# Attention's PSUM as four single banks and two pairs instead of two and three

## The chip, the cores and the metric

The kernel runs on one core of one Trainium2 chip. The metric is the device time of one execution in microseconds (us), as the median of three runs. An execution is 39,685 instructions on five engines that run side by side and wait for each other by semaphores: TensorE (PE in the profile), VectorE (DVE), ScalarE (ACT), GpSimd (POOL) and SyncE (SP, which here issues the transfers).

## The reference

Two layers of a network with four branches are computed for 512 latent and 128 context tokens of width 1024. Each layer is

```
h = modulate(rms_norm(x, g_attn), sh1, sc1)
cb, cc, cv, gq, gk, gv, nq, nk, nv, mq, mkv, mkr, gates = in_project(h, w_in)
y_conv = short_conv(cb, cc, cv)
y_gqa  = banded attention of 8 heads on 2 key heads, with a sink per head
y_na   = neighbourhood attention of 4 heads, with a bias table per head
y_mla  = attention of 4 heads on compressed keys and values
x = x + gt1 * (sum of gate_i * (y_i @ w_branch_i)) @ w_o
x = x + gt2 * relu(modulate(rms_norm(x, g_mlp), sh2, sc2) @ w_ff1)^2 @ w_ff2
```

The keys and values of every attention branch also take in 256 cached tokens. All of it is float32; the outputs are the two normed token sets and the new caches.

## The kernel before

Tokens lie on the free axis (640 of them, worked on in two halves of 320), features on the 128 partitions. Each weight slab of 128 columns is split into a high and a low part, so that a projection of one half is 8 steps of three matmuls (`steps`, L199 to L201: high by high, high by low, low by high), all added up in one PSUM tile of one bank.

PSUM has eight banks. `psum(n1, n2)` (L96) opens two pools for a phase: n1 single banks, from which `bank()` takes a tile named `pr`, and n2 pairs of neighbouring banks, from which `banks2()` takes a tile that the profile calls `S`. A tile that takes over a bank waits until the last instruction that reads the bank's tile before it has ended. All phases but one use eight single banks. The attention phase of each layer (`mixers`, L656) uses two singles and three pairs (L680).

What the attention phase does with them: `attend` (L610) goes through 80 blocks, each one head's 128 queries (16 heads of five blocks, the fifth the context's own). A block passes three places:

- `block_scores` takes a pair and writes the scores into it (L479, L480, or L482 to L484 for the MLA heads). VectorE writes the sink column (L508) and takes the row minimum together with the mask table (L515, or L518 without a table); ScalarE's exponential (L524) is the last to read the pair. GpSimd then divides by the sum (L529). Scores are three blocks ahead.
- `block_T` takes a pair and transposes the block's probabilities into it (L538). ScalarE copies their high part out (L542), VectorE subtracts it for the low part (L545), which is the last read of the pair.
- `pair_pv` takes a single bank for the product of two blocks with the values (L555), read out by ScalarE (L559) and VectorE (L578, L576 or L568). It is called from within a projection, after its third step (L202).

Between them `fill` runs pieces of the projections still to come: half of a block's share between the transposition and the next scores, half after them. Each half projection takes a single bank and is read out by ScalarE (L299, L300 and others) or VectorE. The MLA heads' preparation (L1351, L1362, L1383), the sums of squares (L1220) and their spreading (L1239) take single banks as well. `v_pair` takes a pair for three transpositions of values per layer (L414).

The order on TensorE is that of the program text. On VectorE, ScalarE and GpSimd it is chosen in the attention phase by a scheduler when the program is built, by when it reckons their inputs to be ready; within an engine the order is then fixed, and an instruction that waits holds up all that stand behind it. Which of the free banks a new tile gets is settled there too.

Of the kernel before, what the change touches and what calls it, by code (L numbers as in the profile page):

```python
# [36 lines left out]
# slabs of w_in, 128 columns each (MKR: 32), and of the MLA heads' second projections (HEAD + i);  # L37
# the order in which they are used after GK, GQ, GV
# [4 lines left out]
# gate, first row chunk and number of chunks of its branch's projection; first chunk of y  # L43
# [3 lines left out]
# TensorE time to fill per attention block (GQA, neighbourhood, MLA), and the MLA preparation's steps  # L47
RATE = (2000, 2200, 2000)
PREP = (820, 600, 1200)
# blocks scored ahead; share of a block's filling before the next scores; blocks by which the  # L50
# product with the values lags, and the step of a projection under which it runs
AHEAD, PART, LAG, FRESH = 3, 0.5, 1, 2
# blocks to wait for the inputs of the values' transposition, of the norms' sums, of their spreading
# [12 lines left out]
class Net:  # L66
# [28 lines left out]
    @contextmanager  # L95
    def psum(self, n1, n2=0):  # L96
        """PSUM for one phase: n1 single banks, n2 pairs of banks"""
        self.uid += 1
        with ExitStack() as s:
            pool = lambda name, n: s.enter_context(  # L100
                self.tc.tile_pool(name=f"{name}_{self.uid}", bufs=n, space=PSUM, reuse_waits="tile"))
            self.ps1 = pool("ps1", n1)
            self.ps2 = pool("ps2", n2) if n2 else None
            yield
# [35 lines left out]
    def raw(self):  # L140
        """start the load of the next slab"""
        src, kc, m, tag, eng = self.feed.popleft()
        r = self.wp.tile([P, kc, m], F32, name="raw" + tag, tag="raw" + tag, bufs=2 if tag == "w" else 1)
        self.nc.sync.dma_start(r, src.rearrange("p (k m) -> p k m", k=kc))
        self.raws.append((r, kc, m, tag, eng))

    def prefetch(self, dst=None):
        """split the next slab; start the load of the one after it"""
# [9 lines left out]
        if eng and kc == KC:  # L158
            # in halves, so that no engine is held for long
            for a, e in ((0, nc.gpsimd), (KC // 2, nc.vector)):  # L160
                c = slice(a, a + KC // 2)
                nc.scalar.copy(hi[:, c], raw[:, c])
                e.tensor_tensor(lo[:, c], raw[:, c], _r(hi[:, c]), ALU.subtract)
        else:
            nc.scalar.copy(hi, raw)  # L165
            nc.vector.tensor_tensor(lo, raw, _r(hi), ALU.subtract)  # L166
# [4 lines left out]
    def take(self, ahead=True, dst=None):  # L171
        """the next slab; by default the one after it is split meanwhile"""
        if not self.ready:
            self.prefetch()
        hi, lo, tag = self.ready.popleft()
        if ahead:
            self.look(tag)
        return hi, lo

    def look(self, last="w"):  # L180
        """split what comes next, up to a large slab; never two small ones, which share a buffer"""
# [10 lines left out]
    def steps(self, out, w, x, sl, ks=None):  # L192
        """out += sum_k w[k]^T x[k], both operands split; a step per k, yields its time on TensorE"""
# [32 lines left out]
    def silu(self, pool, a, n):  # L226
        """a <- silu(a), n columns"""
# [15 lines left out]
    def mod_chunk(self):  # L243
        """128 modulation columns of both vectors, on VectorE"""
# [11 lines left out]
    def mod_done(self, l, i0, i1):  # L256
        """add the bias to columns i0..i1; fold the norm's gain into 1 + scale"""
# [10 lines left out]
    def mod_first(self, pool, j, w):  # L268
        """layer 0's first shift and scale, chunk j, on TensorE: rows of both vectors, then columns"""
# [19 lines left out]
    def evac(self, ps, h, raw, rows, scale, perm, ctx0):  # L289
        """a PSUM half -> raw[rows, lat 512 | ... | ctx at ctx0]; perm: grid order (r, b, c) -> (b, r, c)"""  # L290
# [23 lines left out]
    def stage(self):  # L314
        """a staging tile; work put off that reads the tile it takes over runs first"""
# [12 lines left out]
    # work put off: small pieces run between the attention blocks, in order  # L328
# [3 lines left out]
    def drain(self, budget=None, tasks=None):  # L332
        """run work put off: all of it, or up to a budget, or all that these tasks have left"""
# [8 lines left out]
    # the same for work on TensorE: one piece per block, once its inputs have had time to arrive  # L342
# [26 lines left out]
    def q_pair(self, raw, rope):  # L369
        """two heads: per head the stack of q_hi (the head's own rows) and q_lo"""  # L370
# [16 lines left out]
    def k_pair(self, raw, rope):  # L387
        """two heads: per head k_hi and k_lo, each in both halves of the partitions"""
# [17 lines left out]
    def v_pair(self, raw):  # L406
        """two heads, token-major values [V_hi | V_lo]; chunks: lat 0-3, ctx 4, cache 5-6"""
# [18 lines left out]
    def wait(self, begun=0, ended=0):  # L426
        """hold a fill task until so many heads have begun and ended"""
# [3 lines left out]
    def q_prep(self, c, rope, perm, out):  # L431
        """fill task: a query chunk"""
# [40 lines left out]
    # A block is one head's 128 queries. Three parts, run for different blocks at a time:  # L473
    # scores and softmax; transposition of the probabilities; product with the values.
# [11 lines left out]
    def block_scores(self, B):  # L486
# [8 lines left out]
        # the sink is one more column of scores  # L495
# [51 lines left out]
    def pair_pv(self, R):  # L547
        """[V_hi P; V_lo P] of a pair of blocks"""
# [31 lines left out]
    def values_out(self):  # L580
        """the pending product with the values. It takes the bank of the last projection: best soon
        after the next one has begun, which leaves both time to be read out"""
# [5 lines left out]
    def blocks(self, H):  # L588
        """the blocks of a head: latent queries in two pairs, then the context's own"""
# [20 lines left out]
    def attend(self, blocks, fill, budget):  # L610
        """software pipeline over the blocks; projections fill TensorE in between"""
# [32 lines left out]
    def na_table(self, l, head, piece):  # L644
        """a piece of a neighbourhood head's table: BIG outside the column window, less the bias;
        zeros for the cached keys are there already"""
# [8 lines left out]
    def mixers(self, l, first):  # L655
        """first(): the projections of the GQA keys and of the first queries, evacuated here"""  # L656
# [5 lines left out]
        with ExitStack() as s:  # L662
# [17 lines left out]
            self.ps_stack.enter_context(self.psum(2, 3))  # L680
            # the last block's sink column falls on the first key to the right, which the band admits
# [5 lines left out]
            def table(hd):  # L687
                """after a block's scores: the next neighbourhood head's table, as this head's is done with"""
# [32 lines left out]
            def advance():  # L721
                """one step of the current fill task; None when there is none or it has to wait"""
# [80 lines left out]
    def conv(self, l, c):  # L803
# [9 lines left out]
        # u: [0 | lat 512 | 0 0 | ctx 128 | 0]  # L813
# [29 lines left out]
    def merge(self, l, x):  # L843
# [7 lines left out]
        with tc.tile_pool(name="yp", bufs=1, side="right", reuse_waits="tile") as yp:  # L851
            yh = yp.tile([P, 10, NTOK], F32R, name="yh")
            yl = yp.tile([P, 10, NTOK], F32R, name="yl")
            # the branches' outputs pass through the tile that takes x afterwards
# [64 lines left out]
    def boundary(self, l, x, a, dst, g0, nxt, stack):  # L919
        """the last 8 slabs before a norm, one token half after the other, so that the norm of the  # L920
        first half runs under the products of the second; then the first two slabs after the norm"""
# [77 lines left out]
    def start(self):  # L999
        """first norm and first projections, chunk by chunk as the modulation's weights arrive"""  # L1000
# [35 lines left out]
        # rows of the modulation, their columns, the norm and the products, each for an earlier chunk  # L1036
# [54 lines left out]
class Norm:  # L1091
    """RMS norm of the trunk x: sums of squares over the partitions on TensorE, then either the
    modulated, split input of the next products or, with nxt None, the final output"""
# [22 lines left out]
    def stat(self, h):  # L1116
        """reciprocal root of the mean square, tokens on partitions: a column per 128 of them"""
# [9 lines left out]
    def spread(self, h, sbuf=False):  # L1127
        """the same as a row on every partition"""
# [32 lines left out]
    def flush(self):  # L1161
        """the low parts put off by apply()"""
        while self.due:
            self.due.popleft()()

    def second(self, net):
        """the second half's norm under the first half of the next two slabs"""
# [38 lines left out]
class Mla:  # L1206
    """latent attention: compressed queries, keys and values"""
# [5 lines left out]
    def root(self, key, chunks, n):  # L1213
        """1 / root of the mean of squares, tokens on partitions, a column per chunk (tile, first token)"""
# [10 lines left out]
        # an estimate from the exponent, three Newton steps  # L1225
# [8 lines left out]
    def spread(self, key, cols):  # L1234
        """columns of root() -> a bank with the same row on every partition; cols: (column, first, tokens)"""
# [8 lines left out]
    def keys(self):  # L1244
        """compressed keys and values with the cached ones, normalised and split"""
# [33 lines left out]
    def queries(self):  # L1279
        """compressed queries, normalised and split"""  # L1280
# [34 lines left out]
    def rotary(self):  # L1315
        """rotary key in partitions 64..95"""
# [17 lines left out]
    def prep(self, hd):  # L1334
# [5 lines left out]
        # columns: w_uq (two row chunks), w_ukv's keys, and for an even head its pair's values  # L1340
# [57 lines left out]
def _slabs(w, m=P):  # L1398
    """[K, N] -> [N/m, 128, K/128 * m]: per output chunk, the k chunks side by side"""
# [4 lines left out]
def _tokens(lat, ctx):  # L1404
    """[512, F], [128, F] -> [128, F/128 * 640], features on partitions, two halves of lat | ctx"""
# [41 lines left out]
def _rpb(rpb):  # L1447
    """[H, 15, 31] -> [H, 128 (r, c), 384 (rel, kr, kc)]"""
# [84 lines left out]
```

## Time and profile before

| | us |
|---|---|
| median of 3 runs (2402.55 to 2404.66) | 2402.82 |
| span of the profiled execution, first to last instruction | 2405.3 |
| attention phase, layer 0 (74.7 to 404.5) | 329.8 |
| attention phase, layer 1 (1251.4 to 1578.4) | 327.0 |
| TensorE busy | 2315.2 |
| VectorE busy | 1404.0 |
| ScalarE busy | 935.7 |

The page gives no other time of the profiled execution than its span; the span lies 2.5 us (0.1%) above the median of the runs. Matmuls are pipelined: the profile shows one of 320 columns as 309 ns, while the next starts some 147 ns after it. An engine counts as idle only where none of its instructions is under way.

### The profile page before, as it was taken

The page shows a single profiled execution, that of the slowest core. Times are in us where ns is not written, and L with a number is a line of the kernel's source. Part 1 is how long each engine was busy: PE and PEld are TensorE (multiplying, and loading weights), DVE is VectorE, ACT ScalarE, POOL GpSimd, SP SyncE. Part 2 cuts the span into 40 slices and gives each one's busy share as a digit, 9 for nine tenths or more (in the row PEclk, how much of TensorE's full clock was granted, in tenths as well). Part 3 has the DMA queues.
Part 4 walks back from the last instruction along what each step waited for, and adds up shares of the span by engine and source line. Part 5 has one row for each costly group of instructions (what it writes and reads, how often), then busy time and mean ns, then how long its engine had stood idle before and what let it go on. Part 6 is the DMA issues. An engine that isn't in the chain of part 4 may idle for free. (4 is left out here: it accounts for less than half of the span.)

```text
span 2405.3 us, 39685 instructions
## 1 busy us (share of the span) xinstructions
PE 2315.2 (96%) x15766; PEld 2251.6 (94%) x15766; DVE 1404.0 (58%) x2744; ACT 935.7 (39%) x1877; POOL 367.3 (15%) x468
## 2 busy tenths in 40 slices
PE   8899888999999999999999998999999999999998
PEld 4899888999999999999988997899999999999998
DVE  5776676666645777776467767753333454343433
ACT  5555554322224332222255656542222343131311
POOL 0333321111111000000123333211111200000001
PEclk9999999999999999999999999999999999999999
DMA  6323312444431344443331231042222212222222
GB/s 231 96 72 86 91 35 102 167 142 148 151 114 59 132 158 157 147 153 123 97 124 58 83 112 38 25 162 73 82 71 86 90 45 72 78 76 75 79 80 71
DMA packets 85321, 242.96 MB, mean 101 GB/s; under 512 B 9744, under 2 KB 31248, under 8 KB 83728
## 3 DMA queue, kind: packets, MB, share of 16 engines
q1 hardware_dynamic: 85136, 240.43, 30.9%
q8 instruction: 124, 2.03, 0.3%
q14 instruction: 61, 0.50, 0.1%
HBM read 222.14 MB, written 12.75 MB: 98 GB/s over the span
## 5 line engine op out<-in xcount | busy, mean ns | idle before, releaser
L199 PE MATMUL pr<-hhi,whiw 128*128 128x320 f32 (+1 forms) x2752 | 868.4, 316 | 20.5 <-ACT st L300 9.6
L201 PE MATMUL pr<-hhi,wlow 128*128 128x320 f32 (+1 forms) x2752 | 852.7, 310 | 2.3 <-DVE wlow L166 1.4
L200 PE MATMUL pr<-hlo,whiw 128*128 128x320 f32 (+1 forms) x2752 | 853.4, 310 | 0.1
L199 PEld LDWEIGHTS pr<-hhi,whiw 128*128 128x128 f32 (+1 forms) x2752 | 516.4, 188 | 26.9 <-ACT st L300 11.7
L201 PEld LDWEIGHTS pr<-hhi,wlow 128*128 128x128 f32 (+1 forms) x2752 | 515.6, 187 | 5.0 <-DVE wlow L166 2.6
L200 PEld LDWEIGHTS pr<-hlo,whiw 128*128 128x128 f32 (+1 forms) x2752 | 516.7, 188 | 3.4 <-DVE hlo L1159 2.6
L165 ACT CAST whiw<-raww 128x1024 fp32r<-128x1024 f32 x184 | 192.7, 1047 | 286.6 <-PE pr L200 269.4
L166 DVE TENSOR_TENSOR wlow<-raww,whiw 128x1024 fp32r<-128x1024 f32 x184 | 237.1, 1289 | 60.8 <-ACT whiw L165 60.3
L199 PE MATMUL pr<-hh,whiw 128*128 128x320 f32 x832 | 257.0, 309 | 0.0
L200 PE MATMUL pr<-hl,whiw 128*128 128x320 f32 x832 | 256.9, 309 | 0.0
L201 PE MATMUL pr<-hh,wlow 128*128 128x320 f32 x832 | 256.9, 309 | 0.0
L253 DVE SCALAR_TENSOR_TENSOR junk<-wm,cb 128x1024 bf16<-128x1024 f32 x160 | 195.7, 1223 | 46.8 <-DMA wm<-in_wm 43.9
L916 DVE SCALAR_TENSOR_TENSOR x<-pr,mod,x 128x256 f32<-128x256 f32 x320 | 107.7, 379 | 195.1 <-PE pr L201 192.9
L1114 POOL TENSOR_TENSOR sqs<-sqs,sq 128x320 f32<-128x320 f32 x48 | 47.7, 993 | 969.8 <-ACT sq L1112 941.9
L529 POOL TENSOR_SCALAR p<-p,sm 128x512 f32<-128x512 f32 (+3 forms) x160 | 123.2, 771 | 369.5 <-DVE sm L528 299.6
L894 POOL TENSOR_TENSOR acc<-acc,sg 128x320 f32<-128x320 f32 x96 | 89.0, 931 | 521.1 <-DVE sg L893 521.0
L524 ACT ACTIVATE p<-S,sm 128x641 f32<-128x641 f32 (+6 forms) x160 | 112.1, 701 | 139.0 <-DVE sm L515 65.1
L889 ACT ACTIVATE sg<-pr 128x320 f32<-128x320 f32 x128 | 55.5, 437 | 284.1 <-PE pr L201 276.3
L200 PEld LDWEIGHTS pr<-hl,whiw 128*128 128x128 f32 x832 | 156.4, 188 | 0.0
L199 PEld LDWEIGHTS pr<-hh,whiw 128*128 128x128 f32 x832 | 156.4, 188 | 0.0
L201 PEld LDWEIGHTS pr<-hh,wlow 128*128 128x128 f32 x832 | 156.4, 188 | 0.0
L893 DVE SCALAR_TENSOR_TENSOR sg<-sg,pr 128x320 f32<-128x320 f32 x96 | 46.2, 487 | 187.4 <-PE pr L201 187.4
(207 smaller groups left out, 3774.5 us busy)
## 6 DMA issues: line engine op xcount, KB each, us to landing
raww<-in_w SPq DMA_DIRECT2D x128, 512.0 KB, 3.6
wm<-in_wm SPq DMA_DIRECT2D x80, 512.0 KB, 3.7
raww<-in_wg SPq DMA_DIRECT2D x64, 512.0 KB, 3.8
raww<-in_wa SPq DMA_DIRECT2D x42, 512.0 KB, 3.6
wm<-in_wm SPq DMA_DIRECT2D x8, 1024.0 KB, 14.3
raww<-in_wo SPq DMA_DIRECT2D x16, 512.0 KB, 3.6
rawb<-in_wb SPq DMA_DIRECT2D x48, 128.0 KB, 2.1
kt<-kt SPq DMA_DIRECT2D x24, 224.0 KB, 3.2
```

What stands on the lines that cost most here:

```text
L165: nc.scalar.copy(hi, raw)
L166: nc.vector.tensor_tensor(lo, raw, _r(hi), ALU.subtract)
L199: nc.tensor.matmul(out, lhsT=whi[:, kw, :], rhs=xhi[:, kx, sl], start=(i == 0), stop=False)
L200: nc.tensor.matmul(out, lhsT=whi[:, kw, :], rhs=xlo[:, kx, sl], start=False, stop=False)
L201: nc.tensor.matmul(out, lhsT=wlo[:, kw, :], rhs=xhi[:, kx, sl], start=False, stop=(i == n - 1))
L253: nc.vector.scalar_tensor_tensor(self.junk, raw, 1.0, self.cb[v], ALU.mult, ALU.mult, accum_out=self.mod[l]["mod"][:, v, i:i + 1])
L524: nc.scalar.activation(p[:, :B["n"]], B["sc"], AF.Exp, bias=sm[:, 0:1], scale=-1.0, accum_out=sm[:, 1:2])
L529: nc.gpsimd.tensor_scalar(p[:, :n], p[:, :n], sm[:, 1:2], 1.0, ALU.mult, ALU.mult)
L889: nc.scalar.activation(sg, gp[hf][:, :HALF], AF.Tanh, scale=0.5)
L894: nc.gpsimd.tensor_tensor(a, a, sg, ALU.add)
L916: self.nc.vector.scalar_tensor_tensor(x[:, j, o + a:o + b], ps[:, a:b], m[:, v, g0 + j:g0 + j + 1], x[:, j, o + a:o + b], ALU.mult, ALU.add)
L1114: eng.tensor_tensor(self.acc[h], self.acc[h], sq, ALU.add)
```

## The change

One number pair in `mixers` is changed; `psum`, `bank` and `banks2` stay as they are. The other lines of the diff replace comments by empty lines, so that line numbers stay the same; they are left out here.

```diff
             self.ps_stack.close()
-            self.ps_stack.enter_context(self.psum(2, 3))
-            # the last block's sink column falls on the first key to the right, which the band admits
+            self.ps_stack.enter_context(self.psum(4, 2))
+
```

The instructions and their order on TensorE and SyncE are the same as before. On VectorE, ScalarE and GpSimd the scheduler puts some of them in another order. As built, the two pairs go to scores and transpositions in turns, with few exceptions: at 11 places in the first layer and 13 in the second a block's scores take the very pair that the transposition just before them wrote.

VectorE, layer 0, around 155 to 163 us of the trace before. `S_1653` is the pair of a context block's transposition, `S_1659` that of the scores right behind it on TensorE; `st`, `rt`, `tab`, `qt` are staging tiles and tables.

```order
 L515 ISA sm 128x1
-L508 COPY S_1659<-nsink_104 128x1
 L545 TENSOR_TENSOR pt<-S_1653,pt 128x128
-L515 ISA S_1659,sm<-S_1659,tab 128x641
-L515 ISA sm 128x1
-L528 RECIPROCAL sm<-sm 128x1
 L367 TENSOR_TENSOR st<-st,rt 128x512
 L653 TENSOR_TENSOR tab<-tab,rt 128x256
 L528 RECIPROCAL sm<-sm 128x1
-L380 TENSOR_TENSOR qt<-st,qt 64x640
-L578 TENSOR_TENSOR y<-pr,plo 64x256
+L508 COPY S_1659<-nsink_104 128x1
```

The sink column and the minimum of the scores have moved behind the low part of the transposition and behind two other instructions (L367, L653).

VectorE, layer 0, around 374 to 380 us. `S_4256` is the pair of an MLA block's transposition, `S_4291` that of later scores; `kt` and `qt` are keys and queries in preparation.

```order
-L578 TENSOR_TENSOR y<-pr,plo 64x256
-L528 RECIPROCAL sm<-sm 128x1
 L214 TENSOR_TENSOR kt<-kr,kt 32x896
+L528 RECIPROCAL sm<-sm 128x1
 L214 TENSOR_TENSOR qt<-st,qt 96x640
+L578 TENSOR_TENSOR y<-pr,plo 64x256
+L545 TENSOR_TENSOR pt<-S_4256,pt 128x6x128
 L568 TENSOR_TENSOR y<-pr,plo 64x64 x2
 L518 TENSOR_REDUCE sm<-S_4291 128x1
-L545 TENSOR_TENSOR pt<-S_4256,pt 128x6x128
```

The low part of the transposition (L545) has moved ahead of the two L568 and of the later scores' minimum (L518).

## Rows read from the trace of the kernel before

**Rows 1.** Windows: stretch and length; busy of PE, PEld, DVE, ACT, POOL; PEclk; DMA.

```profile
74.70:404.50 329.80, 301.09 (x2102) 285.13 (x2100) 239.54 (x545) 189.84 (x447) 105.99 (x154) 0.96 0.21 63
1251.40:1578.40 327.00, 300.20 (x2103) 284.15 (x2101) 239.55 (x545) 190.42 (x446) 106.07 (x154) 0.96 0.21 64
```

**Rows 2.** Groups by line, PE, 74.7 to 404.5: busy, mean ns, idle before, releasers.

```profile
L199 PE MATMUL pr<-hhi,whiw 128*128 128x320 f32 (+1 forms) x304 | 102.2, 336 | 7.9 <-ACT st L300 4.1 <-DVE y L578 1.8 <-DVE y L568 1.2
...
L555 PE MATMUL pr<-pt,vt 128*128 128x256 f32 (+1 forms) x368 | 52.5, 287 | 3.4 <-DVE vt L214 1.9 <-ACT st L300 0.6 <-DVE y L578 0.6
L538 PE MATMUL S<-ident,p 128*128 128x128 f32 x328 | 50.4, 278 | 4.5 <-issue 2.2 <-ACT p L524 1.2 <-DVE pt L545 1.0
...
L1383 PE MATMUL pr<-whib,kt 128*128 128x128 f32 x14 | 4.5, 321 | 1.9 <-DVE kt L214 1.9
...
L1362 PE MATMUL pr<-kt,whib 128*64 128x512 f32 (+1 forms) x8 | 3.2, 397 | 3.0 <-DVE y L576 1.2 <-ACT st L300 1.1 <-DVE y L578 0.8
...
L1220 PE MATMUL pr<-ones,rt 128*128 128x1 f32 x22 | 2.9, 252 | 2.9 <-POOL rt L1300 1.6 <-DVE y L578 1.3
```

**Rows 3.** The same, 1251.4 to 1578.4.

```profile
L199 PE MATMUL pr<-hhi,whiw 128*128 128x320 f32 (+1 forms) x304 | 102.1, 336 | 8.4 <-ACT st L300 4.0 <-DVE y L578 2.5 <-DVE y L568 1.2
...
L555 PE MATMUL pr<-pt,vt 128*128 128x256 f32 (+1 forms) x368 | 52.3, 286 | 3.4 <-DVE vt L214 1.9 <-ACT st L300 0.6 <-DVE y L578 0.6
...
L1383 PE MATMUL pr<-whib,kt 128*128 128x128 f32 x14 | 4.5, 321 | 2.3 <-DVE kt L214 2.3
...
L1362 PE MATMUL pr<-kt,whib 128*64 128x512 f32 (+1 forms) x8 | 3.1, 394 | 2.3 <-ACT st L300 1.5 <-DVE y L578 0.8
```

**Rows 4.** Timeline near 1486: start, length, engine, line, tiles.

```profile
1485.76 0.54 DVE L214 TENSOR_TENSOR vt<-pr,vt 128x384 fp32r<-128x384 f32 x1
...
1488.34 0.39 PE L1362 MATMUL pr<-kt,whib 128*64 128x512 f32 x1
```

**Rows 5.** Timeline near 89; in brackets idle time before and who ended it.

```profile
88.91 0.22 PE L479 MATMUL S<-kt,qt 128*128 128x128 f32 x1
...
90.91 0.69 ACT L524 ACTIVATE p<-S,sm 128x513 f32<-128x513 f32 x1 [1.98 <-DVE sm L515]
...
91.83 0.63 PE L538 MATMUL S<-ident,p 128*128 128x128 f32 x4 [1.21 <-ACT p L524]
```

**Rows 6.** Timeline near 156 to 163.

```profile
155.87 0.33 PE L479 MATMUL S<-kt,qt 128*128 128x384 f32 x1
...
158.73 0.32 DVE L545 TENSOR_TENSOR pt<-S,pt 128x128 fp32r<-128x128 f32 x1
...
159.19 0.63 PE L538 MATMUL S<-ident,p 128*128 128x128 f32 x4 [0.99 <-DVE pt L545]
...
162.97 0.41 PE L199 MATMUL pr<-hhi,whiw 128*128 128x320 f32 x1 [1.81 <-ACT st L300]
```

**Rows 7.** Timeline near 373 to 380.

```profile
372.80 0.82 PE L538 MATMUL S<-ident,p 128*128 128x128 f32 x6
...
377.61 0.82 PE L538 MATMUL S<-ident,p 128*128 128x128 f32 x6
378.06 0.35 DVE L568 TENSOR_TENSOR y<-pr,plo 64x64 f32<-64x64 f32 x2
...
378.44 0.96 DVE L518 TENSOR_REDUCE sm<-S 128x1 f32<-128x768 f32 x1
...
379.32 0.95 DVE L545 TENSOR_TENSOR pt<-S,pt 128x768 fp32r<-128x768 f32 x1
...
380.41 0.30 PE L482 MATMUL S<-kt,qt 96*128 96x128 f32 x1 [0.67 <-DVE pt L545]
```

**Rows 8.** Timeline near 397 to 398.

```profile
397.02 0.96 DVE L545 TENSOR_TENSOR pt<-S,pt 128x768 fp32r<-128x768 f32 x1 [0.18 <-ACT pt L542]
...
397.99 1.06 PE L538 MATMUL S<-ident,p 128*128 128x128 f32 x6 [1.32 <-issue]
```

**Rows 9.** Windows again: one short stretch.

```profile
108.30:111.80 3.50, 3.50 (x16) 3.50 (x15) 2.33 (x7) 1.78 (x6) 0.69 (x1) 0.51 0.00 0
```

## The prediction

> **What bounds the kernel now.** I read the windows by stage first [rows 1]. In the two attention phases TensorE is busy for 301.1 of 329.8 us and 300.2 of 327.0 us, VectorE for 239.5 us in each. So TensorE sets the time, but in this phase some 28.7 and 26.8 us are lost on it, and VectorE, which reads out most banks, has 73% of the phase full. Only these 656.8 of the span's 2405.3 us use the pools that change; everywhere else the program is the same, and I count nothing there.
>
> Then the groups of TensorE with their idle time and its releasers [rows 2, 3]. Idle time ahead of lines that write `pr` and that ends with a reader of another `pr` tile (ScalarE's `st` L300, VectorE's `y`, `kt` and `vt`) is a wait for a single bank. In the first layer that is L199 7.9, L555 3.4, L1362 3.0, L1383 1.9 and the 1.3 of L1220 that `y` L578 ends: 17.5 us. In the second it is L199 8.4, L555 3.4, L1383 2.3, L1362 2.3: 16.4 us. Together 33.9 us. Ahead of the pairs' transpositions (L538) stand 4.5 us in a layer, of which 1.0 ends with a pair's reader (L545), the rest with probabilities that are late.
>
> **Four single banks.** A tile now takes over the bank of the fourth tile before it instead of the second or the one before. I went through the 226 single-bank tiles of the two phases in the timeline, and compared each one's first matmul with the last read of its new predecessor. None is early: the nearest is an MLA matmul at 1488.34 us whose bank was read out at 1485.76 + 0.54 = 1486.30 us, 2.0 us ahead [rows 4]. So all 33.9 us of these waits can go. Where TensorE only meets something else that is late, less is won; that is counted below, on the other side.
>
> **Two pairs.** A pair tile now takes over the pair of the second tile before it, sometimes of the one just before, instead of the third or second. I did the same comparison for the 162 pair tiles of each layer. In each layer 45 begin before their new predecessor's last read has ended: the first at 88.91 us, 2.7 us too early; the last in layer 0 at 397.99, level with it (397.02 + 0.96 = 397.98), which counts since the release takes some 0.05 us to arrive [rows 5, 8]. The lacks add up to 39.1 us in the first layer and 38.3 in the second: 77.4 us. By kind, in the first layer: 17 scores held by the exponential of the scores before (18.9 us), 17 transpositions held by the low part of the transposition before (9.4), 6 scores held by the transposition just before (6.3), 5 others (4.5).
>
> That sum is an upper bound, and 77.4 - 33.9 = +43.5 us its net. It isn't additive: what makes a pair late is a queue on VectorE or ScalarE, and TensorE runs into the same queue a little later in the trace of before too. Three places, by hand:
>
> At 88.91 the scores would have to wait for the exponential that ends at 90.91 + 0.69 = 91.60, so 2.7 us. But at 91.83 TensorE already stands still for 1.21 us for probabilities from the same engines [rows 5]. Net of that, 1.5 us.
>
> At 155.87 the scores follow a context block's transposition in the same pair; its low part ends at 158.73 + 0.32 = 159.05, so 3.2 us. In before, TensorE stands still at 159.19 for 0.99 us for that very read, and at 162.97 for 1.81 us for a single bank [rows 6]. The 1.81 is in the 33.9 already; the 0.99 comes off: 2.2 us net. The new order on VectorE puts the sink column and the minimum behind that low part, as it must.
>
> At 377.61 the transposition waits for the low part of the one before, which ends at 379.32 + 0.95 = 380.27, so 2.7 us; at 380.41 TensorE stood still for 0.67 us anyway [rows 7]: 2.0 us net. Here the new order helps: the low part is moved ahead of L568 (0.35) and L518 (0.96), some 1.3 us earlier, which leaves 0.7.
>
> The three cost 8.6 us by the plain sum, 5.7 us (66%) net of the waits that are there already, and 4.4 us (51%) with the new order on VectorE. I take 60% of 77.4, near the middle of the two: 46.4 us. As bounds: 100% if each reader keeps its distance behind TensorE's write however long TensorE stood, and 30% if a stall lets VectorE, which is idle for 27% of the phase, work off its queue, so that the following tiles are met in time; the smallest share of the three places is 0.7 of 2.7 (26%).
>
> **The clock.** The granted clock falls to half in short stretches after some waits: 0.51 between 108.3 and 111.8 us, and 0.96 on the mean of each phase [rows 9, 1]. 3.5 us at half clock cost 1.7 us of work. Waits of up to 1.8 us on single banks go [rows 6] and some of 2 to 3 us on pairs come, so I add one or two falls in all: 2.6 us, with 0 and 10 as bounds. The Trainium skill, in "TensorE: Matmul & The Clock Gate", section "A second HAM failure mode: psum-queue depth-cycling", tells of a kernel that cycled through PSUM banks, idled briefly between groups of matmuls, and saw its clock swing between half and full. By that rule the clock would take more than my one or two falls; the trace of before has both the short idle times and the falls, and doesn't tell what more of them bring.
>
> **The sum.** 46.4 - 33.9 + 2.6 = +15.1 us on the profiled execution's 2405.3; its span is 2.5 us above the median of the runs, which doesn't matter for the difference. 2402.8 + 15.1 gives 2418 us.
>
> **The rivals.** *The queues do drain (faster).* With 30% of 77.4 the pairs cost 23.2 us, and 23.2 - 33.9 = -10.7: 2392 us. It decides at 44% (33.9 of 77.4): below that share the kernel is faster. For it: VectorE's idle share, the order that moves low parts ahead, and the third place with its 26%. Against it: two of the three places keep 56% (1.5 of 2.7) and 69% (2.2 of 3.2), and the queues at them are made of work on weights, keys and queries that TensorE's own order sets. A page's rule points this way: the Trainium skill, "Perfetto Trace Analysis", section "Matmuls", wants independent groups of matmuls to rotate through different banks so that reading one out overlaps the next. It holds for the projections, where [rows 2, 3] show the waits that it speaks of; but the scores and transpositions are such groups too, and they lose a pair.
>
> *It comes out even.* At 40 to 48% of 77.4 the net lies between -2.9 and +3.3 us: the waits only change their name, from `pr` to `S`. About 2403 us. For it speaks that both kinds of wait end with the same two engines.
>
> *Nothing drains (much slower).* At 90 to 100% the net is +36 to +43.5 us, and with more falls of the clock (10 us) up to +53: 2439 to 2456. For it: each block needs scores, minimum and exponential one after another in one pair, and with one pair for scores that chain can't overlap the next block's. Against it: the three places.
>
> That the change doesn't do what it says can nearly be left out: TensorE's order stays, and the nearest single bank has 2.0 us to spare.
>
> **How the numbers follow.** Likeliest, 50 to 85% of the pairs' sum: +5 to +34 us, 2407 to 2436, chance 0.57. Nothing drains: 0.13. Even: 0.13. Faster: 0.17. What a measurement of this kernel can tell from no change is some 0.2%, 4.8 us. Slower by more than that is the likeliest and the heavy case, 0.70; within it 0.13; faster 0.17. The range leaves out the outer half of the heavy case and less than half of the faster one: 2394 to 2442.
>
> **What would show it.** Right: ahead of L199, L555, L1362 and L1383 no idle time that ends with a reader of `pr`; ahead of L538, L479 and L482 15 to 25 us in each layer that ends with L524 or L545, against 2.2 ahead of L538 now [rows 2]; at the place of 88.91 some 2.5 us ahead of L479 that end with L524, at that of 155.87 some 3 us that end with L545, and the waits at 91.83 and 159.19 gone. Each attention phase 5 to 17 us longer, all else unchanged. Wrong: waits for `pr` that stay; idle time ahead of the pairs under 12 us a layer (the queues drain) or over 35 (nothing does); a change outside the two phases; or a mean clock in the phases below 0.93, which would make the clock and not the waits the larger term.

## The result, and the profile after

The changed kernel takes 2442.3 us (median of 4 runs, 2437.4 to 2444.2); the kernel before, beside it on the same chip, 2402.9 us. The ratio is 1.0157, with a 95% interval of 1.0142 to 1.0171: 39 us slower, where +15 was forecast, and 0.3 us past the end of the range. The profiled execution's span is 2442.4 us, 37.1 us more than before.

First the windows by stage: the two attention phases, and the two stretches behind them (columns as in [rows 1]).

```profile
75.20:423.20 348.00, 308.92 (x2105) 292.43 (x2104) 237.80 (x545) 190.37 (x447) 102.78 (x154) 0.94 0.19 60
1270.80:1616.20 345.40, 307.08 (x2103) 290.72 (x2102) 237.29 (x545) 190.24 (x446) 102.44 (x154) 0.94 0.19 60
...
423.20:1270.80 847.60, 837.75 (x5693) 832.16 (x5693) 551.80 (x970) 272.04 (x482) 78.69 (x79) 1.00 0.40 138
1616.20:2442.40 826.20, 814.48 (x5545) 811.27 (x5544) 330.10 (x574) 243.25 (x414) 67.25 (x72) 0.99 0.25 82
```

Against [rows 1] the phases are 18.2 and 18.4 us longer, 36.6 of the span's 37.1. The stretches behind them took 846.9 and 826.9 us before, so they stand still. Inside the phases the loss has two parts. TensorE's idle time grew from 28.7 to 39.1 us and from 26.8 to 38.3 us: 21.9 us in all. And TensorE is *busy* for 7.8 and 6.9 us longer with the same matmuls, 14.7 us in all, at a mean granted clock of 0.94 where it was 0.96.

The groups of TensorE in layer 0, which answer to [rows 2]:

```profile
L199 PE MATMUL pr<-hhi,whiw 128*128 128x320 f32 (+1 forms) x305 | 103.5, 339 | 0.0
...
L555 PE MATMUL pr<-pt,vt 128*128 128x256 f32 (+1 forms) x368 | 52.9, 289 | 0.2 <-DVE pt L545 0.2
L538 PE MATMUL S<-ident,p 128*128 128x128 f32 x328 | 51.0, 282 | 7.7 <-DVE pt L545 3.8 <-ACT p L524 2.2 <-POOL p L529 1.6
L479 PE MATMUL S<-kt,qt 128*128 128x256 f32 (+2 forms) x108 | 33.5, 319 | 15.4 <-ACT p L524 10.9 <-DVE pt L545 4.5
...
L482 PE MATMUL S<-kt,qt 96*128 96x512 f32 (+2 forms) x36 | 13.8, 382 | 10.7 <-ACT p L524 9.7 <-DVE pt L545 0.7
...
L1383 PE MATMUL pr<-whib,kt 128*128 128x128 f32 x14 | 3.8, 271 | 0.0
L1362 PE MATMUL pr<-kt,whib 128*64 128x512 f32 (+1 forms) x8 | 3.2, 396 | 0.0
...
L1220 PE MATMUL pr<-ones,rt 128*128 128x1 f32 x22 | 2.7, 244 | 1.0 <-POOL rt L1300 1.0
```

The waits for single banks are gone: L199 7.9 to 0.0, L555 3.4 to 0.2, L1362 3.0 to 0.0, L1383 1.9 to 0.0; the 1.0 left ahead of L1220 ends with GpSimd, not with a reader of `pr`. In their place stand the waits for pairs: ahead of L479, L482 and L538, 31.8 us end with the exponential (L524) or the low part (L545), against 3.5 before: 2.2 ahead of L538 [rows 2] and 1.3 ahead of L479 and L482. (The single bank of [rows 4], with 2.0 us to spare, was the nearest; ahead of L1362 there is indeed nothing.) Layer 1, which answers to [rows 3], has 31.2 us:

```profile
L538 PE MATMUL S<-ident,p 128*128 128x128 f32 x328 | 51.9, 284 | 7.7 <-DVE pt L545 3.7 <-ACT p L524 2.2 <-POOL p L529 1.6
L479 PE MATMUL S<-kt,qt 128*128 128x256 f32 (+2 forms) x108 | 32.9, 314 | 15.8 <-ACT p L524 11.3 <-DVE pt L545 4.4
...
L482 PE MATMUL S<-kt,qt 96*128 96x512 f32 (+2 forms) x36 | 13.5, 376 | 9.8 <-ACT p L524 8.9 <-DVE pt L545 0.7
```

The places of [rows 5 to 7] in the timeline of the changed kernel (in brackets idle time before, and who ended it):

```profile
92.14 0.47 PE L479 MATMUL S<-kt,qt 128*128 128x128 f32 x1 [2.64 <-ACT p L524]
...
95.14 1.27 PE L538 MATMUL S<-ident,p 128*128 128x128 f32 x5
...
159.15 1.40 DVE L366 TENSOR_TENSOR st<-st,cosg 128x512 f32<-128x512 f32 x1
160.47 1.75 DVE L163 TENSOR_TENSOR wlow<-raww,whiw 128x512 fp32r<-128x512 f32 x1
162.14 0.82 DVE L515 CUSTOM_DVE_ANT_0 S<-S,tab 128x641 f32<-128x641 f32 x1
...
162.88 0.28 DVE L545 TENSOR_TENSOR pt<-S,pt 128x128 fp32r<-128x128 f32 x1
...
163.22 0.62 PE L479 MATMUL S<-kt,qt 128*128 128x384 f32 x1 [2.91 <-DVE pt L545]
...
167.06 0.60 PE L538 MATMUL S<-ident,p 128*128 128x128 f32 x4
...
392.87 0.96 DVE L545 TENSOR_TENSOR pt<-S,pt 128x768 fp32r<-128x768 f32 x1
...
394.06 0.82 PE L538 MATMUL S<-ident,p 128*128 128x128 f32 x6
```

92.14 is what stood at 88.91: 2.64 us for the exponential. 163.22 is what stood at 155.87: 2.91 us for the context block's low part. 394.06 is what stood at 377.61, and it doesn't wait: its pair was read out at 393.83. The waits that stood at 91.83 and 159.19 are gone (95.14 and 167.06 have no bracket). The rows of VectorE show what holds the pair up to 163.16: ahead of the minimum (L515) of the block before, the queue has a step of the rotary embedding (L366, 1.40 us) and half of a weight slab's low part (L163, 1.75 us), and the low part that frees the pair stands behind all of them. TensorE, whose order is fixed, stands still behind it.

The granted clock in short windows, ahead of each of these two waits and behind it, where [rows 9] showed one such stretch of before:

```profile
85.00:89.30 4.30, 4.30 (x34) 4.22 (x32) 3.32 (x7) 2.65 (x6) 3.09 (x3) 1.00 0.00 0
91.70:98.30 6.60, 6.16 (x25) 6.12 (x26) 4.09 (x9) 3.37 (x9) 1.06 (x2) 0.50 0.21 74
155.00:160.00 5.00, 5.00 (x38) 4.99 (x36) 3.50 (x10) 2.73 (x8) 1.98 (x3) 1.00 0.01 3
163.40:166.60 3.20, 3.20 (x14) 3.20 (x15) 2.67 (x8) 2.70 (x6) 0.80 (x1) 0.50 0.97 348
```

TensorE runs at 2.4 GHz up to the wait and at 1.2 GHz behind it. In the two phases there are 15 waits of over 1.7 us ahead of `S` that end with L524 or L545, and a stretch at half clock begins within 2 us of the end of 12 of them, a little before it or behind it. In the trace of before, 4 of 9 waits of 1.7 to 1.9 us, all for single banks, have such a stretch. Half clock covers 40.3 and 39.4 us of the two phases, against 23.4 and 23.9 us before.

### The profile page after: what moved, and what is told of

The parts are those of the page before. It is cut to its first block, busy times and chain, and to the rows that moved or that the text cites. A ratio compares the mean times of both kernels' runs of the same rounds, so it can differ in the third digit from the quotient of the medians.

```text
span 2442.4 us, 39683 instructions
## 1 busy us (share of the span) xinstructions
PE 2329.5 (95%) x15766; PEld 2265.1 (93%) x15766; DVE 1400.2 (57%) x2744; ACT 936.0 (38%) x1877; POOL 360.6 (15%) x468
## 5 line engine op out<-in xcount | busy, mean ns | idle before, releaser
L199 PE MATMUL pr<-hhi,whiw 128*128 128x320 f32 (+1 forms) x2752 | 869.7, 316 | 2.7 <-ACT st L300 1.5
L199 PEld LDWEIGHTS pr<-hhi,whiw 128*128 128x128 f32 (+1 forms) x2752 | 518.9, 189 | 4.6 <-ACT st L300 1.7
L199 PE MATMUL pr<-hh,whiw 128*128 128x320 f32 x832 | 257.1, 309 | 0.0
L529 POOL TENSOR_SCALAR p<-p,sm 128x512 f32<-128x512 f32 (+3 forms) x160 | 118.6, 741 | 420.0 <-DVE sm L528 372.4
L524 ACT ACTIVATE p<-S,sm 128x641 f32<-128x641 f32 (+6 forms) x160 | 112.0, 700 | 151.0 <-DVE sm L515 78.8
L199 PEld LDWEIGHTS pr<-hh,whiw 128*128 128x128 f32 x832 | 156.4, 188 | 0.0
```

The source lines that it names most:

```text
L199: nc.tensor.matmul(out, lhsT=whi[:, kw, :], rhs=xhi[:, kx, sl], start=(i == 0), stop=False)
L524: nc.scalar.activation(p[:, :B["n"]], B["sc"], AF.Exp, bias=sm[:, 0:1], scale=-1.0, accum_out=sm[:, 1:2])
L529: nc.gpsimd.tensor_scalar(p[:, :n], p[:, :n], sm[:, 1:2], 1.0, ALU.mult, ALU.mult)
```

## The experiments

Theory: the pairs are late because their last readers stand behind other work in the queues of VectorE and ScalarE, and each long wait then costs clock. Rivals: the new assignment of pairs is to blame (scores that take the pair of the transposition just before them); the length of the chain alone; or the clock is the larger part. All times below are medians of interleaved rounds, with ratios against the kernel before, which took 2403.4 to 2405.3 us beside them.

**Two singles and two pairs.** Takes the pair away without giving the singles.

```diff
-            self.ps_stack.enter_context(self.psum(4, 2))
+            self.ps_stack.enter_context(self.psum(2, 2))
```

> Two singles and two pairs, two banks left unused: the changed kernel without its two further single banks. It tells what the pairs cost by themselves and what the singles give beside them. In the changed kernel TensorE stands still some 33 us in each layer's attention for readers of pairs, and not at all for readers of singles; before, 17.5 and 16.4 us for singles. If the two kinds of wait add up, the singles' 33.9 us come back on top of 2442 us: 2470 to 2480 us, with 12 to 17 us a layer ahead of L199, L555, L1362, L1383. Rival: both kinds end with the same queues on VectorE and ScalarE, and one stall covers the next, so that the waits only divide up: 2442 to 2455 us, with at most 6 us a layer ahead of those lines.

Measured: 2442.5 us, ratio 1.0154 (1.0138 to 1.0169), the same as with four singles. Waits of TensorE in its layer 0 (tile and line, who ended them: us in all, times, longest):

```profile
PE S L479 <- ACT p L524: 9.1, 8, 2.6
PE S L479 <- DVE pt L545: 4.5, 5, 2.9
PE S L482 <- ACT p L524: 4.3, 4, 1.8
PE S L538 <- DVE pt L545: 4.2, 6, 1.2
...
PE pr L555 <- DVE vt L214: 1.9, 1, 1.9
```

With two pairs the waits for singles fall to some 7 us a layer by themselves, from 17.5 in [rows 2]; TensorE now stands still for pairs in their stead. And what two more banks save there is lost again ahead of the pairs: their waits are 25.1 us in this layer, 31.8 with four singles (L482 waits 4.3 us for the exponential here, 9.7 there). So the 33.9 us were no gain of their own.

**A pair of its own for scores and for transpositions.** Tests the assignment: no scores ever take a transposition's pair.

```diff
+    def banks3(self):
+        return self.ps3.tile([P, 1024], F32, name="S2", tag="S3")
...
-        tp = self.banks2()
+        tp = self.banks3()
...
-            self.ps_stack.enter_context(self.psum(4, 2))
+            self.ps_stack.enter_context(self.psum(4, 1, 1))
```

> Four singles, and one pair for scores and one for transpositions, each in a pool of its own, so that scores never take the pair of the transposition just before them. If it matters which pair the scheduler gives, the 4.4 us a layer that end ahead of scores with the low part of a transposition (L545) go, and the time falls by 5 to 12 us, to 2430 to 2437. Rival: with one pair for scores it is the chain scores, minimum, exponential that can't overlap the next scores, however the pairs are given: the waits for L524 (now 20 us a layer) stay or grow, and the time is 2440 to 2455.

Measured: 2459.8 us, ratio 1.0228 (1.0214 to 1.0242), 17.5 us slower still. Waits in its layer 0 (lines after the new function are 4 higher: L483 is L479, L486 is L482, L542 is L538):

```profile
PE S L483 <- ACT p L528: 16.5, 14, 3.8
PE S L486 <- ACT p L528: 11.4, 6, 2.8
PE S L542 <- DVE pt L549: 8.2, 7, 2.3
```

The waits for the exponential grow, as the rival had it, and the time lies above even the rival's range. The assignment falls as a cause: taking turns is better than one pair each.

**Idle matmuls in the waits.** Matmuls into a single bank that nothing reads are put ahead of the 20 tiles of a layer that wait longest (177 in each layer), sized by the waits, to keep the clock up; the readers of the pairs are left as they are.

```diff
+WARM = {7: 17, 13: 5, 29: 15, 43: 18, 58: 13, 84: 4, 88: 7, 94: 6, 117: 4, 119: 4, 120: 10, 121: 10, ...}
...
+        n = WARM.get(self.pairs, 0)
+        self.pairs += 1
+        if n:
+            d, h = self.bank(), self.h[0]
+            for _ in range(n):
+                self.nc.tensor.matmul(d[:, :HALF], lhsT=h[:, 0, 0:P], rhs=h[:, 0, 0:HALF], start=True, stop=True)
```

> The changed kernel with idle matmuls (a product of 320 columns into a single bank that nobody reads) ahead of the 20 pair tiles of each layer before which TensorE stood still over 0.9 us, as many as fit into that wait (4 to 18). They do nothing for the output. If the clock falls because TensorE stands still, the half-clock stretches of the phases (mean clock 0.94) go, and with them most of the 14.7 us by which TensorE's busy time in the phases grew: 2426 to 2434 us at a mean clock of 0.98 or more in the phases. Rival: the falls have another cause, or the waits are longer by what the idle matmuls add: 2440 to 2450 us.

Measured: 2425.3 us, ratio 1.0082 (1.0069 to 1.0096). Its phases:

```profile
75.20:412.50 337.30, 319.99 (x2279) 303.71 (x2277) 237.78 (x545) 189.52 (x446) 103.95 (x154) 0.99 0.20 62
1258.00:1597.30 339.30, 320.78 (x2280) 304.49 (x2280) 238.38 (x546) 190.43 (x449) 104.58 (x154) 0.99 0.20 62
```

The clock is at 0.99, above the 0.96 of the kernel before, and 17 us of the 39 are back with it, though TensorE still can't go on before the pairs are free. So the falls of the clock cost time here. But the 17 us are not the price of the falls that the change added: half clock covers 13 us of these two phases, where the changed kernel has 80 and the kernel before 47. They are what 67 us less of half clock give, some 0.25 us for each; in proportion the 32 us that were added would be worth 8 us, an estimate from these two runs. The growth of the busy time, 14.7 us, lies above that.

**Readers of the pairs first.** The scheduler is told to give the sink column, the minimum, the exponential and the two parts of the transposition precedence on their engines; the split of the banks and TensorE's order stay.

```diff
-            nc.vector.tensor_reduce(mn, sc, AX.X, ALU.min)
+            with self.tc.high_priority(100):
+                nc.vector.tensor_reduce(mn, sc, AX.X, ALU.min)
...
-        self.nc.vector.tensor_tensor(B["lo"], B["src"], _r(B["hi"]), ALU.subtract)
+        with self.tc.high_priority(100):
+            self.nc.vector.tensor_tensor(B["lo"], B["src"], _r(B["hi"]), ALU.subtract)
```

> The changed kernel, in which the scheduler is told to prefer the readers of pairs (sink column, minimum, exponential, high and low part of the transposition) to other work on VectorE and ScalarE by 100 places of the program; TensorE's order is the same. If a pair is late because its readers stand in a queue behind weights, keys and queries, the 33 us a layer ahead of pairs fall by half or more, with some waits for singles in their place: 2405 to 2425 us. Rival: the chain of scores, minimum and exponential itself is too long for one pair (without any queue), or the fixed order can't be bettered: 2435 to 2448 us.

Measured: 2410.2 us, ratio 1.0024 (1.0015 to 1.0033): 32 of the 39 us are back. The same place as at 163 us above, in its timeline (lines are higher by up to 7: L552 is L545, and below L543 is L538, L529 is L524):

```profile
156.84 0.28 DVE L552 TENSOR_TENSOR pt<-S,pt 128x128 fp32r<-128x128 f32 x1
157.04 0.80 DVE L163 TENSOR_TENSOR wlow<-raww,whiw 128x512 fp32r<-128x512 f32 x1
...
157.18 0.44 PE L479 MATMUL S<-kt,qt 128*128 128x384 f32 x1 [1.25 <-DVE pt L552]
```

The weight slab's step (L163) now stands behind the low part, and the wait is 1.25 us instead of 2.91. Its phases, and its waits in layer 0:

```profile
74.00:405.00 331.00, 300.89 (x2108) 283.84 (x2109) 235.62 (x547) 192.03 (x451) 106.40 (x154) 0.97 0.21 64
1249.40:1582.30 332.90, 301.93 (x2106) 285.05 (x2107) 237.27 (x547) 191.78 (x451) 105.84 (x154) 0.96 0.21 64
```

```profile
PE S L543 <- DVE pt L552: 6.8, 7, 2.2
PE S L482 <- ACT p L529: 5.5, 4, 1.8
PE S L479 <- ACT p L529: 4.9, 6, 1.5
PE S L479 <- DVE pt L552: 4.1, 6, 1.5
...
PE S L482 <- DVE pt L552: 1.8, 2, 1.1
```

From 693.4 us the phases are down to 663.9: 16.3 us less idle time and 13.2 us less busy time, with the clock back at 0.97 and 0.96. The scores' wait for the exponential is halved (10.9 + 9.7 to 4.9 + 5.5 us); the transpositions' wait for the low part grows (3.8 to 6.8). All in all 23.1 us of the 31.8 still stand ahead of the pairs, so these waits did not fall by half, as was expected, though the time lies in the range. What is left of idle time, 30.1 and 31.0 us, is near that of the kernel before (28.7 and 26.8), but stands ahead of pairs where it stood ahead of singles.

**The same precedence in the kernel before** (two singles, three pairs), to see whether it is a gain of its own.

> The same preference in the kernel before, with two singles and three pairs. There pairs are hardly waited for (about 5 us a layer), and singles are, 17 us a layer. If what one pool's readers gain the other's lose in the same queues, the waits for singles grow and the time is 2405 to 2420 us. Rival: the preference only removes late probabilities and costs nothing: 2392 to 2404 us.

Measured: 2402.5 us, ratio 0.9996 (0.9985 to 1.0008). No gain: with three pairs the readers' place in the queue makes no difference to the time.

**The same precedence with two singles and two pairs**, to see whether the further singles count once the pairs' waits are short.

> Two singles and two pairs, with the readers of the pairs given precedence as in e5 (2410.2 us with four singles). Theory A, the two further singles count for nothing in this phase: within 5 us of e5, 2405 to 2415. Theory B, they counted for nothing only because TensorE stood still for pairs; once those waits are shorter the single waits of the kernel before (some 17 us a layer) come back: 2425 to 2445, with 10 us or more of idle time a layer ahead of L199, L555, L1362 and L1383 that ends with a reader of a single bank.

Measured: 2419.6 us, ratio 1.0067 (1.0054 to 1.008), 9.4 us above the 2410.2 with four singles. Both theories missed: the singles are worth something then, but little more than a quarter of the 33.9 us that the sum gave them.

**Small tiles in single banks.** Scores of the context blocks and transpositions of up to four chunks fit one bank; they take a single, and the pairs are left to the large tiles.

```diff
-        sc = self.banks2()
+        sc = self.bank() if B["kind"] == "ctx" else self.banks2()
...
-        tp = self.banks2()
+        tp = self.bank() if nb <= 4 else self.banks2()
```

> Four singles and two pairs, but what fits into 512 columns is put into a single bank: the transpositions of up to four chunks (the context blocks and the outer blocks of the banded and neighbourhood heads, 40 of 80 in a layer) and the context blocks' scores (16 of 80). Of 162 pair tiles in a layer 106 are left. If the time of the changed kernel is lost on the number of pair tiles in flight, the pairs' waits (33 us a layer) fall by half or more and the clock recovers with them: 2400 to 2420 us. Rival: the waits move to the singles, which now take 56 more tiles a layer with a nearest distance of only 2.0 us: 2430 to 2445 us, with waits ahead of L199, L555 and L538 that end with readers of single banks.

Measured: 2390.2 us, ratio 0.9937 (0.9925 to 0.9949), below the range that was expected. Of the 31.8 us in layer 0 that TensorE waited ahead of pairs for the exponential or the low part, 9.4 are left, while some 6 us ahead of singles have come in. With idle matmuls in its remaining waits, as above:

> The version with the small tiles in single banks (2390 us), with idle matmuls ahead of the 11 tiles of each layer before which TensorE stood over 0.6 us. It had 17 and 23 us of half clock in the two phases. If the clock falls for such waits only, these go to under 7 us each and the time falls by 8 to 14 us: 2376 to 2383 us. Rival: the falls come from many short waits, or the idle matmuls push other work back: 2386 to 2394 us.

Measured: 2385.6 us, ratio 0.992 (0.9906 to 0.9933): 4.6 us less where 8 to 14 were expected. Half clock falls from 49.5 to 28.6 us over the whole of the profiled executions, so that each us of it taken away gives some 0.2 to 0.3 us (4.6 us by the medians, 7.1 by the two spans), much as in the changed kernel. With the readers first instead, on four singles and two pairs:

> The version with the small tiles in single banks, with the same preference for the readers of scores and transpositions. If queues on VectorE and ScalarE still set its remaining waits: 2372 to 2386 us. Rival: what remains are waits for data (queries and probabilities) and for the projections' readers, which the preference puts back: 2388 to 2402 us.

Measured: 2373.8 us, ratio 0.987 (0.9857 to 0.9884): the fastest of all, 30 us below the kernel before. And this last kernel on two singles and three pairs:

> The changes of e8 (short transpositions and the context's scores in single banks, readers of the pairs first) on the split of the kernel before, two singles and three pairs; e8 with four and two took 2373.8 us. Theory A, the single banks are what is short once the small tiles are moved to them: slower than e8 and than before, 2400 to 2440, with 20 us or more a layer of waits for single banks. Theory B, the third pair is worth as much as the two singles: 2370 to 2385.

Measured: 2537.4 us, ratio 1.0555 (1.054 to 1.0569). Its phases beside those of the kernel with four and two, and its waits in layer 0 (L543 transpositions and L479 scores, now in `pr`):

```profile
73.30:469.60 396.30, 323.13 (x2104) 299.42 (x2105) 243.72 (x547) 192.86 (x450) 107.52 (x154) 0.92 0.18 53
1314.20:1712.30 398.10, 324.85 (x2104) 300.72 (x2105) 244.14 (x547) 193.27 (x451) 107.21 (x154) 0.91 0.18 53
```

```profile
72.00:387.30 315.30, 298.79 (x2105) 286.44 (x2103) 236.72 (x547) 190.52 (x449) 109.58 (x154) 0.96 0.22 67
1240.00:1555.00 315.00, 296.55 (x2120) 284.85 (x2119) 235.97 (x544) 188.12 (x445) 107.67 (x153) 0.97 0.22 67
```

```profile
PE pr L543 <- DVE y L585: 16.0, 11, 3.3
PE pr L479 <- DVE y L575: 6.6, 4, 3.6
```

The waits are for single banks, as the first theory had it, and the size was off by 97 us: the phases are 164 us longer, 111 us of it idle time and 53 us busy time at a clock of 0.92 and 0.91. With the readers first in both, the split of two and three is better by 8 us (2402.5 against 2410.2) where all scores and transpositions take pairs, and worse by 164 where the small ones take singles.

## Why the prediction was right and wrong

*The bound and the place* held: TensorE sets the time, only the two phases moved.

The step that failed is the sum: it credited the waits for singles in full, took one share for all pair tiles, and put the clock at 2.6 us.

*Four single banks* held as a reading: no single-bank tile is early, and all of those waits are gone. It failed as a term of the sum. The first experiment shows that with two pairs most of the 33.9 us would have gone without any further bank, and that giving the banks changes the time by nothing. "Where TensorE only meets something else that is late, less is won" stood in the text, and had to stand in the sum.

*Two pairs* was the right term with the wrong size. The idle time came out at +21.9 us; with 33.9 gone, the pairs and what follows from them cost 55.8 us net, 72% of the 77.4 instead of the 60% taken: 9.4 us of the miss. What failed here is one share for all kinds, read from three places. By kind, in layer 0: scores held by the exponential were 18.9 us of lacks, and their waits came to 20.6 us (10.9 + 9.7); transpositions held by the low part were 9.4 and became 3.8 (40%). Of the 20.6 us, 5.4 stand ahead of four scores where the trace of before shows no lack, so that some 15 of the 18.9 came true and others were added. The largest of these four is an MLA block's, in layer 0, before and after:

```profile
341.14 0.47 PE L1383 MATMUL pr<-whib,kt 128*128 128x128 f32 x1 [1.91 <-DVE kt L214]
...
347.07 0.90 ACT L524 ACTIVATE p<-S,sm 128x768 f32<-128x768 f32 x1 [2.49 <-DVE sm L518]
...
348.88 0.48 PE L482 MATMUL S<-kt,qt 96*128 96x512 f32 x1
```

```profile
359.34 0.95 DVE L518 TENSOR_REDUCE sm<-S 128x1 f32<-128x768 f32 x1
...
361.43 0.79 PE L482 MATMUL S<-kt,qt 96*128 96x512 f32 x1 [2.84 <-ACT p L524]
```

Before, TensorE had stood still for a single bank (1.91 us) and run at half clock, and the exponential of the scores ahead had ended at 347.97, in time for 348.88. After, that wait is gone, the scores ahead are written by 356.13, but VectorE has the low part, a step of the rotary embedding, keys and values in its queue and comes to their minimum at 359.34: the wait for a single bank has come back as one for a pair. The comparison of each tile with its new predecessor could not see that, since it took the times of before as fixed.

A reason why the two kinds differ would be that the readers of a transposition already written catch up while TensorE stands still, whereas the chain of the next scores begins later by as much. That is an argument and not shown: over all blocks of layer 0 the mean time from a tile's last matmul to its last read fell alike, from 2.62 to 2.42 us for scores and from 2.31 to 2.15 us for transpositions. The three places were a poor sample: by themselves they came out at or below the forecast (2.64 and 2.91 us, and none at the third, less the 1.21, 0.99 and 0.67 that vanished: 2.7 net, against 4.4), while the MLA scores (L482), of which none that waits for an exponential was among the three, wait 10.7 us in layer 0.

*The clock* was the other mis-sized term: 2.6 us with bounds of 0 and 10, where the busy time of the same matmuls grew by 14.7 us, 12 us of the miss. With the 9.4 us above that is 21.5 of the 22.0 by which the span's +37.1 exceeds the forecast. This splits the miss by idle and busy time. By the experiments with idle matmuls the added half clock is worth some 8 us (the estimate above), and the rest of the 14.7 would then belong to the pairs; no run separates the two. The trace of before had single-bank waits of 1.8 us of which some began a fall and some didn't, and I counted falls won and lost against each other. But 12 of the 15 long waits that came last 2 to 3 us, and 12 of the 15 go with a fall, against 4 of 9 before. The Trainium skill, in "TensorE: Matmul & The Clock Gate", section "A second HAM failure mode: psum-queue depth-cycling", puts the lost throughput of a kernel that idles briefly between groups of matmuls down to such falls; this trace agrees, with a clock of 0.96 before and 0.94 after, and 17 us given back at 0.99.

*Readings and sums.* The prediction put what is left of the 4.5 us ahead of L538 [rows 2], and the 1.21 us at 91.83 [rows 5], down to probabilities that are late. Of the 4.5 us, 2.2 end with nothing that the profile shows, and the 1.21 us were a wait for a pair already: GpSimd had divided that block's probabilities by 85.53, and with three pairs the transposition takes the pair of the scores whose exponential ended at 91.60. The likeliest case's "+5 to +34 us" leaves the clock's 2.6 us out at the lower end and has them in at the upper. Neither changes what failed.

*The rivals.* The queues did not drain, in part because of their order: where the readers of the pairs come first, 32 us are back and the kernel is slower by 0.24%, near the even case; but 23.1 us in each layer still stand ahead of the pairs. "Nothing drains" came nearest by its time, 2439 to 2456, but not by its mechanism: its idle time was to be over 35 us a layer ahead of the pairs, and 31.8 and 31.2 were found; the clock made up the rest. Of the signs that were to show the step right, the 15 to 25 us a layer and the phases' 5 to 17 us were both exceeded, the latter by little; the mean clock of 0.94 stayed above the 0.93 that was to make the clock the larger term, and by the busy time it isn't: 14.7 against 21.9.

What stays open: why the scheduler puts the weight slab's step ahead of the read that frees a pair was not tried; the new order on VectorE and ScalarE that came with the change was not tested apart from the banks; and whether the 23.1 us a layer that are left with the readers first are chain length or queue was not separated.

## What to carry to other kernels

A bank is worth what the tiles waiting for it make of it: a wait that is taken away at one pool can come back at the other, so don't credit it in full, and count lacks by kind of tile, not with one share for all. Before moving banks between pools, move small tiles to where a small bank is enough, and put the instruction that frees a bank ahead of other work in its engine's queue; here these two made 69 us between two kernels with the same banks. Price a wait of 2 to 3 us on TensorE twice, once as idle time and once as half clock behind it; the second price was some 0.2 to 0.3 us for each us of half clock here, where idle matmuls took half clock away.

## What was unexpected of the hardware

Isolated waits of 1.8 to 2.9 us in a stream of matmuls that otherwise ran at 2.4 GHz came with 3.4 or 6.8 us at 1.2 GHz in 12 of 15 cases; behind the 2.64 us wait that ended at 92.14 us TensorE ran at half clock for 6.3 of such a stretch's 6.8 us. Work whose result nobody reads, 354 matmuls in the waits of both layers, made the kernel 17 us faster.
